# Fourteen pairs of k tiles in place of twelve as seven products each, with other sums and a preparation of four steps

## The chip, the cores and the metric

The kernel runs on one core of one Trainium2 chip. The metric is the time of one execution on the device in microseconds (us), as a median over runs. The profile and the trace come from one further execution with the hardware profiler on. PE is TensorE's matmul, PEld its weight load, DVE is VectorE, ACT is ScalarE, POOL is GpSimd, and SP issues most of the transfers.

## The reference

One decoder layer of 256 tokens and 2048 features in float32: a pair of token mixers (mLSTM and RWKV-7), a cross attention, and a channel mixer. The change lies in the last matrix product, the down projection of the channel mixer:

```python
def conv_glu_ffn(h, w_up, conv_w, conv_b, w_down):
    u = h @ w_up
    uc = conv_b + sum(conv_w[j] * shift_right(u, CONV_WIDTH - 1 - j) for j in range(CONV_WIDTH))
    gate, up = split_cols(uc, (D_FF, D_FF))
    return (jax.nn.gelu(gate, approximate=True) * up) @ w_down
...
h = rms_norm(x, ffn_pre_norm[l])
x = x + rms_norm(conv_glu_ffn(h, ffn_w_up[l], ffn_conv_w[l], ffn_conv_b[l], ffn_w_down[l]), ffn_post_norm[l])
```

The operand of the down projection is 256 x 8192, its weights are 8192 x 2048, and its output is 256 x 2048.

## The kernel before, in words

**Matrix products.** Every float32 operand is split into a high part (a cast to float32r) and a low part (the rest), and a product is made of three: high x high, low x high, high x low. Weights arrive as `raw` tiles of 128x1024 by SP (`Feed.dma`, L428, four buffers). ACT casts the high part (`Feed.hi`, L448, tile `wh`) and DVE subtracts for the low part (`Feed.lo`, L520, tile `wl`), with five buffers of each. All matmuls are issued at L191; nearly all other ACT and DVE instructions pass through the helper `Meter.call`, L68.

**The down projection.** It is two blocks (n = 0 and 1) of 1024 output columns, each over 64 k tiles of 128 rows. A block has four PSUM banks: two halves of 128 tokens by two halves of 512 columns. One k tile costs 4 x 3 = 12 matmuls of 128x512. The operand is kept in `ac`; `asplit` (L1911) splits two k tiles at a time into `as`, first a cast on ACT and then a subtraction on DVE. `as` has two buffers, so the cast for the tiles kk+2 and kk+3 waits until PE is done with the tiles kk-2 and kk-1.

**Pairs.** At the k tiles listed in `SEVEN` (L1906; six in each block) two neighbouring k tiles are multiplied together as a 2x2 by 2x2 product of blocks (two halves of the tokens, two k tiles, two halves of the columns) with seven products in place of eight: `seven_products` (L532) issues 7 x 3 = 21 matmuls in place of 24. Four of them go to extra PSUM banks (`more`), which `join_sums` (L556) combines behind the last pair of a block. The seven products need sums of weights and sums of operands, which `prepare` (L452), a generator, makes in steps. The weights of a pair are loaded to a place of their own (`pair_loads`, L487; `sraw`). That place, the sums `sums` and `f4`, and the joined banks all lie in one SBUF tile, which the trace calls `end`; they are told apart by their shapes and their times. The split sums are the tiles `sa` (of operands), `ts` and `t4` (of weights; the trace calls the last one `t`). `prepare` also overwrites one of the four 512-column quarters of `sraw`, so that the pair's own `wh` and `wl` are split from changed weights.

**Order.** The order of the instructions on each engine is the order in which the code issues them, and each engine works through its own list in that order. For each k tile i, `work` (L577) does the following before it issues the matmuls of tile i:

```python
feed.lo(i + 1 + pair)
...
ahead = b["xs"](k)
if b["seven"]:
    feed.pair_loads(i)
feed.lo(i + 3 + pair)
feed.dma(i + 7 + pair)
if b["seven"]:
    feed.ahead_of_pairs(i)
```

So at tile i the operands for tile i+2 are split (for even i), then the weights of tile i+3 on ACT and on DVE, and behind these comes one step of `prepare` (`ahead_of_pairs`, L492). A pair at tile c is prepared in six steps, one at each of the tiles c-6 to c-1. An entry of `preps` (L402) holds the tile at which the first step is issued.

## Time and profile before

| | |
|---|---|
| runs shown | 1797.34 us median of 3 (1796.83 to 1848.11) |
| profiled execution | 1796.52 us, of which the span of the instructions is 1794.7 us |
| PE busy | 1785.2 us, 99% of the span, 11778 matmuls |
| DVE busy | 1395.6 us, 78% |
| ACT busy | 1076.7 us, 60% |
| granted TensorE clock | 0.999 of full speed, mean |
| down projection | matmuls from 1462.9 us to 1787.0 us |
| transfers of pairs' weights | 24, of 512 KB each |

Matmuls are pipelined, so their durations overlap, and a PE that is busy all the time may still not be at its peak. Times within the text are microseconds from the start of the span; "idle before" is the time in which an engine stood still ahead of an instruction, with the engine whose signal ended it.

### The profile page before, as it was taken

The page shows a single profiled execution, that of the slowest core. Times are in us where ns is not written, and L with a number is a line of the kernel's source. Part 1 is how long each engine was busy: PE and PEld are TensorE (multiplying, and loading weights), DVE is VectorE, ACT ScalarE, POOL GpSimd, SP SyncE. Part 2 cuts the span into 40 slices and gives each one's busy share as a digit, 9 for nine tenths or more (in the row PEclk, how much of TensorE's full clock was granted, in tenths as well). Part 3 has the DMA queues.
Part 4 walks back from the last instruction along what each step waited for, and adds up shares of the span by engine and source line. Part 5 has one row for each costly group of instructions (what it writes and reads, how often), then busy time and mean ns, then how long its engine had stood idle before and what let it go on. Part 6 is the DMA issues. An engine that isn't in the chain of part 4 may idle for free.

```text
span 1794.7 us, 30098 instructions
## 1 busy us (share of the span) xinstructions
PE 1785.2 (99%) x11778; PEld 1629.7 (91%) x11778; DVE 1395.6 (78%) x2020; ACT 1076.7 (60%) x1616; POOL 28.9 (2%) x51
## 2 busy tenths in 40 slices
PE   9999999999999999999999999999999999999998
PEld 9999988888888999999999999999999998888887
DVE  7869995766665767778878777877777778888887
ACT  7576454654554666677566667666655655556554
POOL 0100000000100000000000000000000000000000
PEclk9999999999999999999999999999999999999999
DMA  8755564454556676656666666666666676767664
GB/s 283 206 170 186 164 190 146 125 180 144 200 188 211 227 243 186 190 150 197 208 203 198 203 209 192 199 206 204 199 200 209 192 229 213 227 186 227 209 209 129
DMA packets 99134, 351.59 MB, mean 196 GB/s; under 512 B 10896, under 2 KB 13968, under 8 KB 98864
## 3 DMA queue, kind: packets, MB, share of 16 engines
q1 hardware_dynamic: 97888, 347.38, 61.3%
q8 instruction: 92, 1.51, 0.3%
q0 software_dynamic: 384, 1.18, 0.2%
q10 hardware_dynamic: 720, 1.12, 0.2%
q14 instruction: 50, 0.41, 0.1%
HBM read 347.01 MB, written 2.10 MB: 195 GB/s over the span
## 4 chain that ended last, share of the span: by engine, by line
PE 99%; DVE 0%; DMA 0%; ACT 0%; issue 0%; SPq 0%; DVEq 0%; ACTq 0%
PE fm L191 55%; PE tm L191 37%; PE more L191 2%; PE gram L191 0%; PE Y L191 0%; PE lv L191 0%; DMA op<-in_op_dram 0%; PE X L191 0%; PE num L191 0%; PE zwa L191 0%; PE U L191 0%; PE gramA L191 0%; PE xo L191 0%; PE zg L191 0%; PE Tn L191 0%; PE mT L1472 0%
## 5 line engine op out<-in xcount | busy, mean ns | idle before, releaser
L520 DVE TENSOR_TENSOR wl<-raw,wh 128x1024 fp32r<-128x1024 f32 (+1 forms) x617 | 741.5, 1218 | 128.6 <-ACT wh L448 125.9
L448 ACT CAST wh<-raw 128x1024 fp32r<-128x1024 f32 (+1 forms) x617 | 633.6, 1044 | 112.7 <-PE tm L191 61.7
L191 PE MATMUL fm<-fx,wh 128*128 128x512 f32 (+1 forms) x2240 | 672.8, 364 | 0.6 <-DVE fx L68 0.4
L191 PE MATMUL fm<-fx,wl 128*128 128x256 f32 x2048 | 558.3, 273 | 0.0
L191 PEld LDWEIGHTS fm<-fx,wh 128*128 128x128 f32 x2240 | 409.3, 190 | 49.9 <-DVE fx L68 1.0
L191 PEld LDWEIGHTS fm<-fx,wl 128*128 128x128 f32 x2048 | 393.3, 192 | 0.0
L191 PE MATMUL tm<-wh,as 128*128 128x512 f32 x856 | 254.8, 379 | 0.0
L191 PE MATMUL tm<-wh,hx 128*128 128x512 f32 (+1 forms) x832 | 243.9, 378 | 1.4 <-ACT hx L68 1.4
L191 PEld LDWEIGHTS tm<-wh,as 128*128 128x128 f32 x856 | 161.7, 189 | 23.2 <-DVE as L68 0.3
L68 ACT COPY ul<-fm 128x256 f32<-128x256 f32 x128 | 44.9, 373 | 225.5 <-PE fm L191 225.5
L191 PE MATMUL fm<-hx,wh 128*128 128x256 f32 x1024 | 174.5, 277 | 0.0
L191 PEld LDWEIGHTS tm<-wh,hx 128*128 128x128 f32 x832 | 151.0, 189 | 21.8 <-POOL wh L507 1.6
L191 PE MATMUL tm<-wl,as 128*128 128x512 f32 x428 | 162.2, 379 | 0.0
L191 PEld LDWEIGHTS fm<-hx,wh 128*128 128x128 f32 x1024 | 155.6, 192 | 1.1
L191 PE MATMUL tm<-wl,hx 128*128 128x512 f32 (+1 forms) x416 | 152.5, 373 | 0.4 <-DVE wl L520 0.3
L68 DVE TENSOR_TENSOR us<-fm,ul 128x256 f32<-128x256 f32 x128 | 48.5, 420 | 131.2 <-ACT ul L68 131.2
L191 PE MATMUL fm<-hx,wl 128*128 128x256 f32 x512 | 140.8, 275 | 0.0
L68 ACT CAST as<-ac 128x512 fp32r<-128x512 f32 x64 | 39.4, 617 | 118.8 <-PE tm L191 118.8
L191 PEld LDWEIGHTS fm<-hx,wl 128*128 128x128 f32 x512 | 98.3, 192 | 0.0
L191 PEld LDWEIGHTS tm<-wl,as 128*128 128x128 f32 x428 | 80.9, 189 | 11.5
L191 PEld LDWEIGHTS tm<-wl,hx 128*128 128x128 f32 x416 | 77.5, 189 | 11.2 <-DVE wl L520 0.5
L191 PE MATMUL fm<-mg,wh 128*128 128x512 f32 (+1 forms) x320 | 84.9, 340 | 0.0
(406 smaller groups left out, 2114.8 us busy)
## 6 DMA issues: line engine op xcount, KB each, us to landing
raw<-in_w_fw_dram SPq DMA_DIRECT2D x232, 512.0 KB, 4.3
raw<-in_w_in_dram SPq DMA_DIRECT2D x160, 512.0 KB, 3.7
raw<-in_w_fd_dram SPq DMA_DIRECT2D x104, 512.0 KB, 4.1
raw<-in_w_br_dram SPq DMA_DIRECT2D x32, 512.0 KB, 4.2
raw<-in_w_mw_dram SPq DMA_DIRECT2D x24, 512.0 KB, 4.8
raw<-in_w_fu_dram SPq DMA_DIRECT2D x24, 512.0 KB, 4.0
end<-in_w_fd_dram SPq DMA_DIRECT2D x24, 512.0 KB, 3.6
raw<-in_w_mo_dram SPq DMA_DIRECT2D x8, 512.0 KB, 4.1
```

The lines of the kernel that those rows point to most:

```text
L68: return f(out, *a, **k)
L191: pe.matmul(out, lhsT, rhs, start=start, stop=stop, skip_group_check=True)
L448: nc.scalar.copy(o, v)
L520: nc.vector.tensor_sub(o, v, h)
```

## The change

Three things change, all within the down projection. The reading of the other parts of the program is not touched.

**Pairs.** `SEVEN` goes from six places in each block to seven: 12, 18, 26, 34, 42, 48, 56 and 10, 16, 24, 32, 40, 46, 54. Before, neighbouring pairs were 8 or 10 k tiles apart; now they are 8 apart, or 6 apart at four places (12 to 18 and 42 to 48, 10 to 16 and 40 to 46).

**Other sums.** The seven products are formed from other sums of the same quarters. Two sums of weights are made by one DVE operation of 1024 elements with a broadcast operand; the quarter that is overwritten is the first one, by a sum that needs that operation's result. The products are issued in another order. `join_sums` has two copies on ACT, not one, and four operations on DVE as before.

**Preparation.** It has four steps in place of six, issued at the tiles c-5 to c-2 where there is room, and at c-4 to c-1 where the pair ahead is 6 tiles away (`last + 2`). The first step makes the overwritten quarter, and an assertion says that the pair's weights must not be split before it.

The three places below show the stretch behind the first pair (tiles 12 and 13) of the first block, up to the next pair. Before, the next pair is at tile 20; in the changed kernel it is at tile 18. The numbers behind the names are those of buffers.

DVE before, from the weights of tile 17 (`wl_16088`) to the split of the operands' sums (`sa_16136`): `end` are sums of the preparation of pair 20, `as` operands, `wl_16152` the weights of tile 20.

```order
L520 TENSOR_TENSOR wl_16088<-raw_16009,wh_16086 128x1024
L68 TENSOR_TENSOR end_15830<-end_15830 128x512
L68 TENSOR_TENSOR end_15830<-ac_10740 128x256
L520 TENSOR_TENSOR wl_16106<-raw_16030,wh_16104 128x1024
L68 TENSOR_TENSOR end_15830<-end_15830 128x512
L68 TENSOR_TENSOR end_15830<-ac_10740,end_15830 128x128 x2
L68 TENSOR_TENSOR as_16125<-ac_10740,as_16125 128x512
L520 TENSOR_TENSOR wl_16130<-raw_16056,wh_16128 128x1024
L68 TENSOR_TENSOR end_15830<-end_15830 128x512
L520 TENSOR_TENSOR wl_16152<-end_15830,wh_16150 128x1024
L68 TENSOR_TENSOR end_15830<-end_15830 128x512
L68 TENSOR_TENSOR sa_16136<-end_15830,sa_16135 128x512
```

DVE now, from the first step of the preparation of pair 18, just behind the weights of tile 17, to the split of the operands' sums (`sa_16142`); `wl_16105` and `wl_16134` are the weights of tiles 18 and 19, `ts` the split of two sums of weights.

```order
L68 TENSOR_TENSOR end_15830<-end_15830 128x1024
L68 TENSOR_TENSOR end_15830<-end_15830 128x512
L519 TENSOR_TENSOR wl_16105<-end_15830,wh_16103 128x1024
L68 TENSOR_TENSOR end_15830<-end_15830 128x512
L68 TENSOR_TENSOR end_15830<-ac_10740 128x256
L68 TENSOR_TENSOR as_16128<-ac_10740,as_16128 128x512
L519 TENSOR_TENSOR wl_16134<-end_15830,wh_16132 128x1024
L68 TENSOR_TENSOR end_15830<-end_15830,ac_10740 128x128
L68 TENSOR_TENSOR end_15830<-ac_10740,end_15830 128x128
L68 TENSOR_TENSOR ts_16112<-end_15830,ts_16111 128x1024
L519 TENSOR_TENSOR wl_16160<-raw_16053,wh_16158 128x1024
L68 TENSOR_TENSOR sa_16142<-end_15830,sa_16141 128x512
```

Before, three steps of sums stand ahead of the first weights of the pair (`wl_16152`), and `sa` follows them with one more sum between. Now the first weights of the pair come directly behind the first step, and `sa` stands behind the weights of tile 20.

ACT in the same stretch before: `wh_16128` is tile 19, `wh_16150` tile 20, `wh_16179` tile 21.

```order
L448 CAST wh_16086<-raw_16009 128x1024
L448 CAST wh_16104<-raw_16030 128x1024
L68 CAST as_16125<-ac_10740 128x512
L448 CAST wh_16128<-raw_16056 128x1024
L68 CAST sa_16135<-end_15830 128x512
L448 CAST wh_16150<-end_15830 128x1024
L68 CAST ts_16158<-end_15830 128x1024
L68 CAST as_16175<-ac_10740 128x512
L448 CAST wh_16179<-end_15830 128x1024
```

And now: `wh_16083` is tile 17, `wh_16103` and `wh_16132` are the pair's tiles 18 and 19, `wh_16158` is tile 20.

```order
L450 CAST wh_16083<-raw_16009 128x1024
L450 CAST wh_16103<-end_15830 128x1024
L68 CAST ts_16111<-end_15830 128x1024
L68 CAST as_16128<-ac_10740 128x512
L450 CAST wh_16132<-end_15830 128x1024
L68 CAST t4_16113<-end_15830 128x512
L68 CAST sa_16141<-end_15830 128x512
L450 CAST wh_16158<-raw_16053 128x1024
```

The pair's first weights, `wh_16103`, are now the second instruction behind the operands of tile 16, and the cast of the operands' sums (`sa_16141`) stands ahead of the weights of tile 20.

PE at the pair, with what each matmul waits for. Before, from the first product of pair 20:

```order
L191 MATMUL more<-wh,as 128x512 [waits Activation_49]
L191 MATMUL more<-wh,as 128x512 [waits DVE_49]
L191 MATMUL more<-wl,as 128x512
L191 MATMUL tm<-wh,as 128x512 [waits Activation_49]
L191 MATMUL tm<-wh,as 128x512
L191 MATMUL tm<-wl,as 128x512 [waits DVE_49]
L191 MATMUL more<-wh,sa 128x512 x2
L191 MATMUL more<-wl,sa 128x512
L191 MATMUL tm<-wh,sa 128x512 x2
L191 MATMUL tm<-wl,sa 128x512
L191 MATMUL more<-ts,sa 128x512 x2
L191 MATMUL more<-ts,sa 128x512 [waits DVE_49]
```

Now, from the first product of pair 18:

```order
L191 MATMUL tm<-wh,as 128x512 [waits Activation_49]
L191 MATMUL tm<-wh,as 128x512 [waits DVE_49]
L191 MATMUL tm<-wl,as 128x512 [waits DVE_49]
L191 MATMUL more<-wh,as 128x512 x2
L191 MATMUL more<-wl,as 128x512
L191 MATMUL tm<-wh,sa 128x512 [waits Activation_49]
L191 MATMUL tm<-wh,sa 128x512 [waits DVE_49]
L191 MATMUL tm<-wl,sa 128x512
L191 MATMUL more<-wh,sa 128x512 x2
L191 MATMUL more<-wl,sa 128x512
L191 MATMUL more<-ts,sa 128x512 x6
L191 MATMUL tm<-t_16113,as 128x512 x2
```

In both, the first two products use the plain operands `as`, and the third is the first that uses `sa`. Now that third product waits for ACT (the high part of `sa`) and then for DVE (the low part).

The diff:

```diff
--- before.py
+++ after.py
@@ -393,12 +393,13 @@
             a, g = blocks[0]["srcs"], blocks[1]["srcs"]
             self.src = a[:LEAD] + [c for p in zip(a[LEAD:], g) for c in p] + g[len(a) - LEAD:]
             self.src += [s for b in blocks[2:] for s in b["srcs"]]
-            n, self.pairs, self.preps = sum(len(b["srcs"]) for b in blocks[:2]), {}, []
+            n, self.pairs, self.preps, self.summed = sum(len(b["srcs"]) for b in blocks[:2]), {}, [], set()
             for b in blocks[2:]:
                 if b["seven"]:
                     for k in b["seven"]["at"]:
                         self.pairs[n + k], self.pairs[n + k + 1] = 0, 1
-                        self.preps.append([n + k - 6, self.prepare(n + k, k), n + k, []])
+                        last = self.preps[-1][2] if self.preps else 0
+                        self.preps.append([max(n + k - 5, last + 2), self.prepare(n + k, k), n + k, []])
                 n += len(b["srcs"])
             self.raw, self.st, self.nd, self.ns, self.nl, self.nop = {}, {}, 0, 0, 0, 0
 
@@ -442,6 +443,7 @@
         def hi(self, upto):
             while self.ns <= min(upto, len(self.src) - 1):
                 self.dma(self.ns)
+                assert self.pairs.get(self.ns) != 0 or self.ns in self.summed
                 r = self.raw[self.ns]
                 wh = self.staged("wh", r)
                 for o, v in self.pieces(self.ns, wh, r):
@@ -451,30 +453,27 @@
 
         def prepare(self, c, k):
 
-            raw, t, f = M["sraw"], M["sums"], M["f4"]
-            (b11, b12), (b21, b22) = ([raw[:, i, j * 512:j * 512 + 512] for j in range(2)] for i in range(2))
+            raw, t, f = M["sraw"].rearrange("p i (j n) -> p (i j) n", j=2), M["sums"], M["f4"]
             x = acpair(k).rearrange("p k (t s) -> p (k t) s", t=2)
-            dve.tensor_add(t[:, 0:512], b22, b12)
+            dve.tensor_add(t[:, 0:1024].rearrange("p (j n) -> p j n", j=2), raw[:, 0:1].broadcast_to((P, 2, 512)), raw[:, 1:3])
+            dve.tensor_add(raw[:, 0], t[:, 0:512], raw[:, 2])
+            self.summed.add(c)
+            yield
+            dve.tensor_add(t[:, 1024:], raw[:, 0], raw[:, 3])
             dve.tensor_sub(f[:, 0:2], x[:, 1:2].broadcast_to((P, 2, P)), x[:, 0:4:3])
-            yield
-            dve.tensor_sub(b12, b12, b11)
-            dve.tensor_sub(f[:, 2], x[:, 0], f[:, 1])
-            dve.tensor_sub(f[:, 3], x[:, 2], f[:, 2])
-            yield
-            dve.tensor_add(t[:, 512:1024], b22, b12)
-            sa = [T2("sa", [P, 4, P], F32R) for _ in range(2)]
-            M["sa"].append(sa)
-            act.copy(sa[0], f)
-            yield
-            dve.tensor_sub(t[:, 1024:], b21, t[:, 512:1024])
-            dve.tensor_sub(sa[1], f, sa[0])
             ts, t4 = [C("ts", f"bg{j}", [P, 1024], F32R) for j in range(2)], [T2("t4", [P, 512], F32R) for _ in range(2)]
             M["ts"].append((ts, t4))
             act.copy(ts[0], t[:, 0:1024])
             yield
+            dve.tensor_sub(f[:, 2], f[:, 1], x[:, 0])
+            dve.tensor_add(f[:, 3], x[:, 2], f[:, 2])
             dve.tensor_sub(ts[1], t[:, 0:1024], ts[0])
+            sa = [T2("sa", [P, 4, P], F32R) for _ in range(2)]
+            M["sa"].append(sa)
             act.copy(t4[0], t[:, 1024:])
-            yield
+            act.copy(sa[0], f)
+            yield
+            dve.tensor_sub(sa[1], f, sa[0])
             dve.tensor_sub(t4[1], t[:, 1024:], t4[0])
             yield
 
@@ -539,13 +538,13 @@
         half = lambda w, c: [v[:, 0, c * 512:c * 512 + 512] for v in w]
         tops = lambda c: [v[:, c * 512:c * 512 + 512] for v in t]
         old, more = banks, sv["more"]
-        for n, (o, x, w) in enumerate(((more[0], [v[:, 0] for v in a], half((w0h, w0l), 0)),
-                                       (old[0], [v[:, 2] for v in a], half((w1h, w1l), 0)),
-                                       (more[2], [v[:, 1] for v in sa], half((w0h, w0l), 1)),
-                                       (old[1], [v[:, 3] for v in sa], half((w1h, w1l), 1)),
-                                       (more[3], [v[:, 0] for v in sa], tops(0)),
-                                       (more[1], [v[:, 2] for v in sa], tops(1)),
-                                       (old[2], [v[:, 3] for v in a], t4))):
+        for n, (o, x, w) in enumerate(((old[1], [v[:, 2] for v in a], half((w1h, w1l), 1)),
+                                       (more[0], [v[:, 0] for v in a], half((w0h, w0l), 1)),
+                                       (old[0], [v[:, 3] for v in sa], half((w1h, w1l), 0)),
+                                       (more[1], [v[:, 2] for v in sa], half((w0h, w0l), 0)),
+                                       (more[2], [v[:, 1] for v in sa], tops(0)),
+                                       (more[3], [v[:, 0] for v in sa], tops(1)),
+                                       (old[3], [v[:, 3] for v in a], t4))):
             wh, wl = (turns(v) for v in w)
             mm(o, x[0], wh, start=new and o in more, stop=False)
             mm(o, x[1], wh, start=False, stop=False)
@@ -557,13 +556,14 @@
 
         more, s = sv["more"], [M["join"][:, i] for i in range(4)]
         sv["sums"] = s
-        act.copy(s[0], more[0])
-        dve.tensor_add(s[2], s[0], more[1])
-        yield
-        dve.tensor_add(s[1], s[2], more[2])
-        dve.tensor_add(s[2], s[2], more[3])
-        yield
-        dve.tensor_add(s[3], s[1], more[3])
+        act.copy(s[1], more[0])
+        dve.tensor_add(s[3], s[1], more[1])
+        yield
+        act.copy(s[0], more[2])
+        dve.tensor_sub(s[0], s[0], s[3])
+        dve.tensor_sub(s[3], s[3], more[3])
+        yield
+        dve.tensor_add(s[2], s[0], more[3])
         yield
 
     def run():
@@ -1903,7 +1903,7 @@
         fu = block("fm", W("w_fw", f - 6), fu_xs(f), fw_evac(f), cols=256, wide=lambda k: M["fx"][:, :, k])
 
     M["as"], M["a4"], M["sa"], M["ts"] = {}, [], [], []
-    SEVEN = [12, 20, 30, 38, 48, 56], [10, 18, 28, 36, 46, 54]
+    SEVEN = [12, 18, 26, 34, 42, 48, 56], [10, 16, 24, 32, 40, 46, 54]
 
     def acpair(e):
         return M["ac"][e // 16][:, e % 16:e % 16 + 2] if e < 32 else M["ac"][2 + (e - 32) // 8][:, e % 8:e % 8 + 2]
```

## The prediction

> **What bounds the kernel now.** I read the page first, then the busy times of the down projection's two blocks.

> ```profile
> PE 1785.2 (99%) x11778; PEld 1629.7 (91%) x11778; DVE 1395.6 (78%) x2020; ACT 1076.7 (60%) x1616; POOL 28.9 (2%) x51
> PE 99%; DVE 0%; DMA 0%; ACT 0%; issue 0%; SPq 0%; DVEq 0%; ACTq 0%
> 1463.08:1624.00 160.92, 160.92 (x748) 140.91 (x747) 135.92 (x168) 96.09 (x120) 0.00 (x0) 1.00 0.69 217
> 1624.00:1777.60 153.60, 153.60 (x713) 134.52 (x712) 132.89 (x164) 92.53 (x119) 0.00 (x0) 1.00 0.64 199
> ```

> The first row gives each engine's busy time, the second the shares of the chain that ended last. The others are stretches: length, then busy us of PE, PEld, DVE and ACT with counts, POOL, the granted clock, DMA. PE is busy in 160.92 of 160.92 us and in 153.60 of 153.60, at clock 1.00: it waits for nobody, so here a matmul less is time less, and any wait that appears is time more. DVE is busy 135.92 / 160.92 = 84% and 87%, which is not much room for engines that depend on each other.

> What a matmul costs comes from the chain, in which PE's runs are merged:

> ```profile
> 1498.05 16.19 PE tm L191 x75
> ```

> 16.19 / 75 = 0.216 us from one matmul to the next (the 379 ns of one matmul overlap). A k tile takes 12 x 0.216 = 2.59 us, a pair 21 x 0.216 = 4.53.

> **What the change removes.** Two pairs more, three matmuls each: 6 x 0.216 = 1.30 us less PE. That is all that PE gains. It has fourteen pairs for certain: the order has 21 matmuls at each.

> **What it adds to DVE.** The added pairs bring their sums and splits. Their prices:

> ```profile
> L68 DVE TENSOR_TENSOR end<-end x48: 680/684/687, 1481.4 to 1755.7; 128x512 f32<-128x512 f32 x48
> L68 DVE TENSOR_TENSOR end<-ac,end x24: 280/288/294, 1484.1 to 1751.8; 128x128 f32<-128x128 f32 x24
> L68 DVE TENSOR_TENSOR end<-ac x12: 415/418/421, 1482.0 to 1749.4; 128x256 f32<-128x256 f32 x12
> L68 DVE TENSOR_TENSOR sa<-end,sa x12: 680/683/686, 1488.9 to 1756.3; 128x512 fp32r<-128x512 f32 x12
> L68 DVE TENSOR_TENSOR ts<-end,ts x12: 1217/1219/1221, 1491.8 to 1759.2; 128x1024 fp32r<-128x1024 f32 x12
> L68 DVE TENSOR_TENSOR t<-end,t x12: 681/684/686, 1494.1 to 1761.5; 128x512 fp32r<-128x512 f32 x12
> ```

> Before, a pair costs 4 x 0.684 + 2 x 0.288 + 0.418 + 0.683 + 1.219 + 0.684 = 6.32 us of DVE. Now two of the four sums are one operation of 1024 elements. The trace has none such on `end`; by the row of `ts` it takes 1.22 us, against 1.37 for two. Its broadcast operand should not matter: an addition of 256 elements with a broadcast operand is in the 0.418 row, at the price that its size gives beside 0.288 for 128 and 0.684 for 512. So a pair now costs 6.17 us, 14 of them 86.3 against 75.8 us. Spread over the stage that would be hidden (DVE idles some 45 us in it). It is not spread: over six k tiles, a pair included, PE needs 4.53 + 4 x 2.59 = 14.9 us, and DVE 6 x (1.22 + 0.34) for the tiles' `wl` and half an `as` plus 6.17, 15.5 us. At the four places where pairs are 6 apart DVE has no slack left, so the order of its work there decides.

> **The walk between two pairs.** The stretch of the trace in which the two pairs at tiles 12 and 20 are prepared shows how the engines are geared:

> ```profile
> 1494.00 0.59 PE L191 MATMUL more<-wh,as 128*128 128x512 f32 x2
> 1495.08 0.41 PEld L191 LDWEIGHTS more<-wh,sa 128*128 128x128 f32 x2
> 1498.54 0.59 PE L191 MATMUL tm<-wh,as 128*128 128x512 f32 x2
> ```

> ```profile
> 1498.73 0.62 ACT L68 CAST as<-ac 128x512 fp32r<-128x512 f32 x1 [1.97 <-PE tm L191]
> 1499.26 1.99 ACT L448 CAST wh<-raw 128x1024 fp32r<-128x1024 f32 x2
> 1503.91 0.62 ACT L68 CAST as<-ac 128x512 fp32r<-128x512 f32 x1 [2.67 <-PE tm L191]
> 1504.44 1.04 ACT L448 CAST wh<-raw 128x1024 fp32r<-128x1024 f32 x1
> 1505.39 0.61 ACT L68 CAST sa<-end 128x512 fp32r<-128x512 f32 x1
> 1507.37 1.05 ACT L68 CAST ts<-end 128x1024 fp32r<-128x1024 f32 x1 [0.41 <-DVE end L68]
> ```

> ```profile
> 1499.39 0.69 DVE L68 TENSOR_TENSOR as<-ac,as 128x512 fp32r<-128x512 f32 x1 [1.17 <-ACT as L68]
> 1500.33 1.23 DVE L520 TENSOR_TENSOR wl<-raw,wh 128x1024 fp32r<-128x1024 f32 x1 [0.26 <-ACT wh L448]
> 1501.48 0.68 DVE L68 TENSOR_TENSOR end<-end 128x512 f32<-128x512 f32 x1
> 1502.08 0.42 DVE L68 TENSOR_TENSOR end<-ac 128x256 f32<-128x256 f32 x1
> 1502.41 1.22 DVE L520 TENSOR_TENSOR wl<-raw,wh 128x1024 fp32r<-128x1024 f32 x1
> 1504.15 0.61 DVE L68 TENSOR_TENSOR end<-ac,end 128x128 f32<-128x128 f32 x2
> 1504.68 0.69 DVE L68 TENSOR_TENSOR as<-ac,as 128x512 fp32r<-128x512 f32 x1
> 1506.66 0.68 DVE L68 TENSOR_TENSOR end<-end 128x512 f32<-128x512 f32 x1
> ```

> The first fence is PE: pair 12 starts at 1494.00 and ends at 1498.54. The cast of the operands for tile 16 starts 0.19 behind that end, because its buffer is released by it; everything on ACT and DVE is queued behind it. DVE reaches the first step of the next preparation at 1501.48, 2.94 us behind the end of the pair. From one DVE instruction to the next, with no wait between, are 1.14 us for 1024 elements, 0.60 for 512, 0.33 for 256; on ACT 0.95 for 1024 and 0.52 for 512 (1504.44 to 1505.39, 1503.91 to 1504.44). A signal between ACT and DVE takes 0.04 (1506.66 + 0.68 = 1507.34, the cast of `ts` starts at 1507.37); an instruction that needs the one ahead of it on DVE starts some 0.03 behind its end (two of 0.288 in 0.61).

> Now the changed order behind pair 12, in us after its end; nothing up to 2.94 is changed. First step: sum of 1024 at 2.94, then the overwritten quarter, which needs it, from 4.19 to 4.87. The pair's first weights (tile 18) may be cast only now: ACT stands idle from 1.76, casts `wh` from 4.91 to 5.95, and DVE, which has `wl` of tile 18 next in its list, stands idle from 4.87 to 5.99. Behind it come the sums of 512 at 7.13 and 256 at 7.73, and `as` of tile 18 at 8.07 (its cast stands behind those of `wh` and `ts`: 6.80 to 7.42). `wl` of tile 19 runs from 8.67, the two operand sums from 9.81 to 10.42. Only then can ACT cast `sa`: 10.46 to 11.07, and behind it `wh` of tile 20: 10.98 to 12.02. DVE has `wl` of tile 20 next, 12.06 to 13.28, and the low part of `sa` behind that, 13.20 to 13.88.

> PE is at pair 18 at 4 x 2.59 = 10.37. The weight load of the low `sa` is the second of the third product. In pair 12 the two loads of that product start at 1495.08, 1.08 us into the pair, and the second 0.22 later: it is due at 10.37 + 1.30 = 11.67. It can start at 13.92. **PE stands 2.25 us**, where it stood for nothing before. The low `t4` follows at 13.80 to 14.48, while PE needs it at its seventh product, at 10.37 + 18 x 0.216 + 2.25 = 16.5: no second wait. Nor is there a debt to the next pair: tile 20 starts at 17.15, `wl` of tile 22 ends near 17.4, and the next cast of operands waits for PE again, as at 1498.73.

> The other three places (42 to 48, 10 to 16, 40 to 46) have the same rows in the same order. At the pairs 8 apart the first step stands at c-5, with a k tile more of time. By the same walk, the low `sa` is ready 0.7 us before those pairs start, 2 us before it is due. Four places cost 4 x 2.25 = 9.0 us.

> The price of one place is bounded so. If each link were at its shortest (no 0.03 and 0.04, the 1024 sum at 1.14, no overlap lost), it would be 1.8; with another 0.3 us of lateness at the first step, 2.6. Zero is excluded by nothing but the walk, and is a rival.

> **Edits at no cost.** The loads of a pair:

> ```profile
> 1488.43 0.33 SPq L487 DMA_DIRECT2D end<-in_w_fd_dram  x1
> 1491.93 0.33 SPq L487 DMA_DIRECT2D end<-in_w_fd_dram  x1
> DMA to landing us min/median/max: 3.4/3.6/6.7
> ```

> They are issued when the `wl` of the pair ahead have read the place; in the new order that is no later, and 1491.93 + 3.6 = 1495.5 is 6.0 us ahead of the step that needs them (2.9 with the slowest landing). SP's queue stands behind them for the same two events as before; four more loads are pair loads, four fewer `raw`. The second copy in `join_sums` (0.58 us on ACT) and the new order of its sums lie behind a block's last pair, where ACT idles 2.2 us a cycle; uncovered, both copies would cost 1.2 us. The first products of a pair now need the weights of its second tile, ready at 9.89 of 10.37; if late, that would add to a wait that comes anyway.

> **Sum.** -1.30 + 9.0 = +7.7 us. From the profiled execution's 1796.52 (span 1794.7) that gives 1804.2. The runs shown lie at 1796.83 and 1797.34, 0.3 to 0.8 above it; with 0.5 added I predict 1804.7 us, and for this case alone 1803 to 1806.5.

> **Rivals.** (a) *The wait is covered*, and only the six matmuls count: 1796.52 + 0.5 - 1.30 = 1795.7 us. The place is the low `sa`; the gain decides if it is ready by 11.67, 2.25 us before the walk has it. For it: DVE idles 1.17 us ahead of 1499.39, and PE has had no wait in twelve preparations. Against: that idle time lies ahead of the cast that PE releases and can't be used, and in all twelve the pair ahead was 8 tiles away or more. (b) *Part of the wait*, 1 us a place, if ACT or DVE gets through the list faster where they wait for each other: +2.7, 1799.7 us. The walk has DVE idle for 1.1 us ahead of `wl` of tile 18 and 0.6 ahead of that of tile 20; these are the only links that could shrink so. (c) *A wait drags the clock down.* PE's rows show

> ```profile
> 1789.00:1792.00 3.00, 0.93 (x2) 0.10 (x1) 1.59 (x4) 0.58 (x1) 0.00 (x0) 1.00 0.69 252
> 1792.00:1794.70 2.70, 0.00 (x0) 0.00 (x0) 0.00 (x0) 0.00 (x0) 0.00 (x0) 0.67 0.31 114
> 7.76 0.95 PE L191 MATMUL tm<-wh,hx 128*128 128x296 f32 x4 [1.38 <-ACT hx L68]
> 5.00:10.00 5.00, 3.53 (x23) 2.75 (x22) 3.15 (x9) 2.57 (x7) 1.16 (x2) 1.00 1.00 377
> ```

> The clock falls to 0.67 in the last stretch, some 2 us after PE's last matmul; a wait of 1.38 us left it at 1.00. If each wait of 2.25 us put the other 16 matmuls of its pair (3.5 us) at 0.67, each would cost 1.7 us more: +6.8, 1811.5 us. [...]

> **How the numbers follow.** The forecast 0.66, (a) 0.15, (b) 0.15, (c) 0.04. The range, 1795.2 to 1807.5, holds the forecast with four waits of up to 2.6 us and a run's own spread, (b) and (a); (c) is left out. All cases lie within 1% of the time before, well inside the 2% that a measurement of this kernel can about tell from no change: faster 0.01, same 0.98, slower 0.01, the outer two for causes that I don't see.

> **What would show it.** PE has 11772 matmuls. In the list of PE's waits four new ones on DVE's `sa`, near 2.2 us each, at tiles 18 and 48 of the first block and 16 and 46 of the second, and none at the ten other pairs. ACT waits some 3 us for DVE's `end` ahead of the first `wh` of these pairs. If these waits are missing or below 1 us, the walk is wrong in the links between ACT and DVE; if they are there and the time isn't longer, my price for the matmuls is.

## The result, and the profile after

| | before | changed |
|---|---|---|
| median of 6 runs | 1796.83 us | 1808.91 us (1805.82 to 1811.2) |
| ratio | | 1.0066, interval 1.0051 to 1.0081 |
| profiled execution, span | 1796.52, 1794.7 us | 1806.3, 1804.2 us |

One of the six runs before was a slow one, at 1848.11 us, and the ratio leaves it out.

The changed kernel is slower, by 9 to 14 us. The prediction, 1804.7 us in a range of 1795.2 to 1807.5, had the direction of its number right and the size too small: the median lies above the range. The six runs fall into two groups, three at 1805.8 to 1806.8 and three at 1811.0 to 1811.2. That there are groups turns out to be the part that the prediction had put aside.

The page after, first the span and the busy times, then the waits of PE in the whole span (us in total, times, longest):

```profile
span 1804.2 us, 30109 instructions
PE 1786.8 (99%) x11772; PEld 1629.4 (90%) x11772; DVE 1406.4 (78%) x2026; ACT 1081.2 (60%) x1624; POOL 28.6 (2%) x51
```

```profile
PE tm L191 <- DVE sa L68: 7.6, 4, 1.9
PE tm L191 <- ACT hx L68: 1.8, 1, 1.8
```

PE has the six matmuls less, and four new waits on DVE's `sa`. The same place as in the prediction, behind the first pair, on DVE and then on ACT:

```profile
1499.77 0.69 DVE L68 TENSOR_TENSOR as<-ac,as 128x512 fp32r<-128x512 f32 x1 [1.17 <-ACT as L68]
...
1501.86 1.94 DVE L68 TENSOR_TENSOR end<-end 128x1024 f32<-128x1024 f32 x2
1504.91 1.23 DVE L519 TENSOR_TENSOR wl<-end,wh 128x1024 fp32r<-128x1024 f32 x1 [1.11 <-ACT wh L450]
...
1509.05 0.29 DVE L68 TENSOR_TENSOR end<-ac,end 128x128 f32<-128x128 f32 x1
...
1510.97 1.22 DVE L519 TENSOR_TENSOR wl<-raw,wh 128x1024 fp32r<-128x1024 f32 x1 [0.50 <-ACT wh L450]
1512.11 0.68 DVE L68 TENSOR_TENSOR sa<-end,sa 128x512 fp32r<-128x512 f32 x1
```

```profile
1503.83 1.04 ACT L450 CAST wh<-end 128x1024 fp32r<-128x1024 f32 x1 [3.15 <-DVE end L68]
...
1509.37 0.62 ACT L68 CAST sa<-end 128x512 fp32r<-128x512 f32 x1 [1.56 <-DVE end L68]
1509.90 1.04 ACT L450 CAST wh<-raw 128x1024 fp32r<-128x1024 f32 x1
```

Pair 12 ends at 1498.92 here (the cast that it releases starts 0.20 later, at 1499.12). Counted from there, the first step starts at 2.94, ACT casts the pair's first weights at 4.91, and the low `sa` runs from 13.19 to 13.87. The prediction had 2.94, 4.91 and 13.20 to 13.88.

What the prediction lacked shows on PE. Two of the four pairs, from the second product to the seventh:

```profile
1509.93 0.59 PE L191 MATMUL more<-wh,as 128*128 128x512 f32 x2
...
1512.85 0.48 PE L191 MATMUL tm<-wh,sa 128*128 128x512 f32 x1 [1.90 <-DVE sa L68]
...
1514.71 2.46 PE L191 MATMUL more<-ts,sa 128*128 128x512 f32 x6
1517.02 0.81 PE L191 MATMUL tm<-t,as 128*128 128x512 f32 x3
...
1588.89 0.59 PE L191 MATMUL more<-wh,as 128*128 128x512 f32 x2
...
1591.81 0.48 PE L191 MATMUL tm<-wh,sa 128*128 128x512 f32 x1 [1.90 <-DVE sa L68]
...
1594.29 0.81 PE L191 MATMUL tm<-t,as 128*128 128x512 f32 x3
```

Without a wait, five products lie between these two starts, 5 x 3 x 0.216 = 3.24 us. The second of the pairs takes 1594.29 - 1588.89 = 5.40, so its wait costs 2.16 us. The first takes 7.09: 2.16 and another 1.69. Its six matmuls on `ts` take 2.46 us, where the same six took 1.46 before, at pair 12:

```profile
1496.59 1.46 PE L191 MATMUL more<-ts,sa 128*128 128x512 f32 x6
```

The stretches of time around them (length, busy us of PE, PEld, DVE, ACT and POOL with counts, granted clock, DMA) say why:

```profile
1509.00:1512.80 3.80, 1.95 (x10) 1.36 (x8) 3.27 (x6) 3.43 (x5) 0.00 (x0) 1.00 0.91 355
1512.80:1514.00 1.20, 1.15 (x4) 0.96 (x5) 1.20 (x3) 0.55 (x1) 0.00 (x0) 0.72 0.76 123
1514.00:1515.00 1.00, 1.00 (x4) 0.82 (x3) 1.00 (x1) 0.00 (x0) 0.00 (x0) 0.50 0.76 307
1515.00:1516.00 1.00, 1.00 (x4) 0.73 (x4) 1.00 (x2) 0.00 (x0) 0.00 (x0) 0.50 0.17 70
1516.00:1517.00 1.00, 1.00 (x4) 0.86 (x3) 0.27 (x1) 0.00 (x0) 0.00 (x0) 0.63 0.84 160
1517.00:1518.50 1.50, 1.50 (x8) 1.32 (x7) 0.00 (x0) 0.58 (x2) 0.00 (x0) 1.00 0.82 284
1590.00:1596.00 6.00, 4.19 (x19) 3.70 (x20) 5.39 (x7) 3.12 (x5) 0.00 (x0) 1.00 0.69 206
```

The granted clock was at 0.50 behind the first wait, from 1513.3 (the second row's mean of 0.72 is 1.00 up to there and 0.50 behind) to 1516.7: 3.41 us in the trace's record, so 1.7 us of work lost. Behind the second wait it stayed at 1.00.

So the profiled execution adds up: -1.30 for the matmuls, 4 x 2.16 = +8.64, +1.69 for the clock, and +0.4 by which the down projection starts later (the wait on `hx` at the kernel's start was 1.8 us, 1.4 before): +9.4, against 1804.2 - 1794.7 = +9.5 us.

### The profile page after: what moved, and what is told of

The parts are those of the page before. It is cut to its first block, busy times and chain, and to the rows that moved or that the text cites. A ratio compares the mean times of both kernels' runs of the same rounds, so it can differ in the third digit from the quotient of the medians.

```text
span 1804.2 us, 30109 instructions
## 1 busy us (share of the span) xinstructions
PE 1786.8 (99%) x11772; PEld 1629.4 (90%) x11772; DVE 1406.4 (78%) x2026; ACT 1081.2 (60%) x1624; POOL 28.6 (2%) x51
## 4 chain that ended last, share of the span: by engine, by line
PE 98%; DVE 1%; ACT 0%; DMA 0%; issue 0%; SPq 0%; DVEq 0%; ACTq 0%
PE fm L191 55%; PE tm L191 36%; PE more L191 2%; PE gram L191 0%; PE Y L191 0%; DMA op<-in_op_dram 0%; PE lv L191 0%; PE X L191 0%; PE num L191 0%; ACT wh L450 0%; PE zwa L191 0%; PE U L191 0%; PE gramA L191 0%; PE xo L191 0%; PE zg L191 0%
## 5 line engine op out<-in xcount | busy, mean ns | idle before, releaser
L191 PE MATMUL fm<-fx,wh 128*128 128x512 f32 (+1 forms) x2240 | 672.8, 364 | 0.6 <-DVE fx L68 0.4
L191 PE MATMUL fm<-fx,wl 128*128 128x256 f32 x2048 | 558.3, 273 | 0.0
L191 PEld LDWEIGHTS fm<-fx,wh 128*128 128x128 f32 x2240 | 409.3, 190 | 49.9 <-DVE fx L68 1.0
L191 PEld LDWEIGHTS fm<-fx,wl 128*128 128x128 f32 x2048 | 393.2, 192 | 0.0
L191 PE MATMUL tm<-wh,as 128*128 128x512 f32 x828 | 246.5, 379 | 0.0
L191 PE MATMUL tm<-wh,hx 128*128 128x512 f32 (+1 forms) x832 | 243.9, 378 | 2.0 <-ACT hx L68 1.8
L68 ACT COPY ul<-fm 128x256 f32<-128x256 f32 x128 | 44.8, 373 | 225.2 <-PE fm L191 225.2
L191 PEld LDWEIGHTS tm<-wh,as 128*128 128x128 f32 x828 | 156.4, 189 | 22.5 <-DVE as L68 0.3
L191 PE MATMUL fm<-hx,wh 128*128 128x256 f32 x1024 | 174.5, 277 | 0.0
L191 PEld LDWEIGHTS tm<-wh,hx 128*128 128x128 f32 x832 | 151.1, 189 | 22.6 <-POOL wh L506 2.0
L191 PE MATMUL tm<-wl,as 128*128 128x512 f32 x414 | 156.9, 379 | 0.0
L191 PEld LDWEIGHTS fm<-hx,wh 128*128 128x128 f32 x1024 | 155.5, 192 | 1.1
L191 PE MATMUL tm<-wl,hx 128*128 128x512 f32 (+1 forms) x416 | 152.5, 373 | 0.0
L68 DVE TENSOR_TENSOR us<-fm,ul 128x256 f32<-128x256 f32 x128 | 48.4, 420 | 131.2 <-ACT ul L68 131.2
L191 PE MATMUL fm<-hx,wl 128*128 128x256 f32 x512 | 140.8, 275 | 0.0
L191 PEld LDWEIGHTS fm<-hx,wl 128*128 128x128 f32 x512 | 98.3, 192 | 0.0
L68 ACT CAST as<-ac 128x512 fp32r<-128x512 f32 x64 | 39.4, 617 | 95.6 <-PE tm L191 95.6
L191 PEld LDWEIGHTS tm<-wl,as 128*128 128x128 f32 x414 | 78.2, 189 | 11.1
L191 PEld LDWEIGHTS tm<-wl,hx 128*128 128x128 f32 x416 | 77.5, 189 | 10.7 <-DVE wl L519 0.3
L191 PE MATMUL fm<-mg,wh 128*128 128x512 f32 (+1 forms) x320 | 84.9, 340 | 0.0
```

The lines of the kernel that those rows point to most:

```text
L68: return f(out, *a, **k)
L191: pe.matmul(out, lhsT, rhs, start=start, stop=stop, skip_group_check=True)
```

## The experiments

Theory 1: the waits come from the order of the two lists at the four places 6 tiles apart, and the rest of the loss from the clock. The rivals: the other sums or products cost by themselves; six tiles are too few for DVE. Differences below are between the medians of the kernel and of the kernel before on the same chip.

**All pairs 8 apart, seven in each block.** The changed kernel with

```diff
-    SEVEN = [12, 18, 26, 34, 42, 48, 56], [10, 16, 24, 32, 40, 46, 54]
+    SEVEN = [8, 16, 24, 32, 40, 48, 56], [6, 14, 22, 30, 38, 46, 54]
```

> The changed kernel with its fourteen pairs set 8 k tiles apart everywhere (8, 16, ... 56 and 6, 14, ... 54); sums and steps as changed. Theory 1 (the waits come from the four places 6 tiles apart, where the preparation starts a tile late): no wait of PE on sa, no clock at 0.5 inside the work, and the time of before less six matmuls of 0.216 us, -1.3 us (+-0.6). Theory 2 (the other sums or the new order of products make PE wait, wherever the pairs stand): waits on sa remain at several pairs, and the time is above that of before.

Measured: 1797.59 us (1796.26 to 1800.06), +0.8, and not -1.3. No wait on `sa`, but another one, in the profiled execution of 1800.06 us:

```profile
PE tm L191 <- ACT wh L450: 1.0, 1, 1.0
PE tm L191 <- DVE wl L519: 0.6, 1, 0.6
```

Both are at the second block's first pair, tile 6. On DVE, the first step of its preparation stands in the midst of the first block's results (`z` and the sums read from `tm`), and the weights of that pair behind them:

```profile
1629.89 0.68 DVE L68 TENSOR_TENSOR z<-end 128x512 f32<-128x512 f32 x1
1630.50 1.23 DVE L519 TENSOR_TENSOR wl<-raw,wh 128x1024 fp32r<-128x1024 f32 x1
1631.64 1.95 DVE L68 TENSOR_TENSOR end<-end 128x1024 f32<-128x1024 f32 x2
1633.51 0.68 DVE L68 TENSOR_TENSOR end<-tm,end 128x512 f32<-128x512 f32 x1
...
1637.39 0.68 DVE L68 TENSOR_TENSOR z<-end 128x512 f32<-128x512 f32 x1
1637.99 1.22 DVE L519 TENSOR_TENSOR wl<-end,wh 128x1024 fp32r<-128x1024 f32 x1
```

The clock fell as well, to 0.50 from 1643.9 to 1647.3 us; one stretch of it:

```profile
1644.00:1646.00 2.00, 2.00 (x6) 1.61 (x5) 2.00 (x4) 1.21 (x2) 0.00 (x0) 0.50 0.73 236
```

In this execution it also fell at the kernel's start, from 8.9 to 12.3 us. So the expectation failed by a new wait of my own making; the places that were to be tested were silent. The clean form of it is the next.

**All pairs 8 apart, none where a block is drained.** Seven and six pairs:

```diff
-    SEVEN = [12, 18, 26, 34, 42, 48, 56], [10, 16, 24, 32, 40, 46, 54]
+    SEVEN = [8, 16, 24, 32, 40, 48, 56], [10, 18, 26, 34, 42, 50]
```

> The changed kernel with all pairs 8 tiles apart, seven in the first block (8 to 56) and six in the second (10 to 50), so that no pair of the second block is prepared while the sums of the first block are still drained, as it was at tile 6. Theory 1: no wait of PE on ACT or DVE in the down projection and no lost clock; thirteen pairs, three matmuls less than before, -0.65 us (+-0.4), all executions within 1 us of each other. Rival (pairs 8 apart wait as well, and tile 6 was only the place where it showed): waits on sa or wl at other pairs, slower than before.

Measured: 1795.91 us (1795.57 to 1796.44), -0.81, and PE waits for nothing in the down projection. Theory 1 holds; a pair 8 tiles behind another waits nowhere.

**The twelve old places.** The changed kernel with `SEVEN` as before:

> The changed kernel with the twelve places of before; sums, order of products and the four steps as changed. Theory 1: no wait, twelve pairs, so the time of before within 0.6 us; DVE is some 12 x 0.15 = 1.8 us less busy than before, which nobody waits for. Theory 2 (sums or products cost by themselves): slower than before by over 1 us, with a wait that the trace names.

Measured: 1796.8 us, +0.04 (ratio 1.0, 0.999 to 1.001), no wait. The other sums, the new order of products and the four steps cost nothing by themselves. One part of the expectation was wrong: over the 314.6 us of the stage, DVE is no less busy, although it has twelve instructions fewer. The row of this kernel, and that of the kernel before:

```profile
1463.30:1777.90 314.60, 314.60 (x1459) 275.40 (x1458) 269.42 (x319) 189.40 (x241) 0.00 (x0) 1.00 0.65 209
```

```profile
1463.08:1777.68 314.60, 314.60 (x1460) 275.43 (x1458) 268.89 (x331) 188.61 (x239) 0.00 (x0) 1.00 0.66 208
```

**Operand sums one step earlier.** The changed kernel at its own fourteen places; in `prepare` the last two sums of operands go from the third step to the second, and the low `sa` from the fourth to the third, ahead of `ts`:

```diff
 dve.tensor_sub(f[:, 0:2], x[:, 1:2].broadcast_to((P, 2, P)), x[:, 0:4:3])
+dve.tensor_sub(f[:, 2], f[:, 1], x[:, 0])
+dve.tensor_add(f[:, 3], x[:, 2], f[:, 2])
...
-dve.tensor_sub(f[:, 2], f[:, 1], x[:, 0])
-dve.tensor_add(f[:, 3], x[:, 2], f[:, 2])
-dve.tensor_sub(ts[1], t[:, 0:1024], ts[0])
 sa = [T2("sa", [P, 4, P], F32R) for _ in range(2)]
 M["sa"].append(sa)
-act.copy(t4[0], t[:, 1024:])
 act.copy(sa[0], f)
-yield
+act.copy(t4[0], t[:, 1024:])
 dve.tensor_sub(sa[1], f, sa[0])
+dve.tensor_sub(ts[1], t[:, 0:1024], ts[0])
+yield
```

> The changed kernel at its own places; the last two sums of operands are made one step earlier, and the split of sa follows one step earlier, ahead of the weights of tile 20. Walked in the same way as in the prediction (us behind the end of the pair ahead): operand sums done 8.7, sa cast 8.7 to 9.3, wl of tile 19 9.2 to 10.4, low sa 10.3 to 11.0, due 11.67. Theory 1 (only the place of sa in the two lists is late): no wait on sa, none of over 0.3 us on wl of the pair, -1.3 us against before (+-0.6). Theory 3 (six tiles are too few for DVE's 15.5 us of work, wherever sa stands): the wait moves to wl or ts and stays above 1 us at each of the four places, so slower than before by 3 us or more.

Measured: 1795.46 us (1795.07 to 1796.27; before 1796.32 to 1797.44 in 31 runs), -1.30, no wait of PE at all in the stage. The row that decides, on DVE behind the first pair, which ends at 1498.78 here:

```profile
1509.23 0.69 DVE L68 TENSOR_TENSOR sa<-end,sa 128x512 fp32r<-128x512 f32 x1
```

That is 10.45 to 11.14 behind the pair, where 10.3 to 11.0 was expected and 11.67 is due. The rival that six tiles are too few for DVE has fallen: the same work at the same places fits when the two operand sums, the cast of `sa` and the split of `sa` stand higher in the lists.

**Six steps at the new places.** The kernel before with only `SEVEN` changed.

> The kernel before (its sums, its products, its six steps) with only the fourteen new places. The first step of a pair 6 tiles behind another is issued at that pair itself, two tiles ahead of where the four steps start. By the walk, sa is ready at 8.2 us behind the pair ahead, due at 11.7, wl of the pair's second tile at 9.9 of 10.6. Theory 1 (the late start and the order of the four steps make the wait): no wait on sa, -1.3 us against before (+-0.6). Theory 3 (six tiles are too few for the work): waits at the four places, slower than before by 2 us or more.

Measured: 1795.19 us (1794.67 to 1796.12), -1.57, no wait. The places alone are harmless too. It takes both, the places 6 apart and the four steps that start two tiles later there with `sa` at their end.

**`sa` ahead of the weights of tile 20.** The changed kernel; at the tile ahead of a pair, the step comes first:

```diff
+if b["seven"] and i + 1 in feed.pairs:
+    feed.ahead_of_pairs(i)
 feed.lo(i + 3 + pair)
```

> The changed kernel, but at the tile ahead of a pair the step of the preparation is issued ahead of the weights of tile 20, not behind them; only the four places 6 tiles apart differ. By the walk the low sa is ready at 12.2 us, not 13.9, due 11.67: PE is late by 0.5 us at each place. Theory 1: four waits on sa of under 0.6 us, no clock at 0.5 inside the work, -1.3 + 4 x 0.5 = +0.7 us against before (+-0.6). Rival: the wait stays above 1.5 us, since something other than the list's order holds sa back.

Measured: 1797.61 us (1796.46 to 1797.91), +1.06. The waits of the weight loads and of PE:

```profile
PEld tm L191 <- DVE sa L68: 2.3, 4, 0.6
PE tm L191 <- DVE sa L68: 0.7, 4, 0.2
```

The loads are late by 0.6 us four times, as the walk has it (0.5). Moving that step past one instruction is worth 8.4 us, the lost clock included (1806.05 of the changed kernel on the same chip, below, against 1797.61).

**The same with a longer wait.** At the four places the split of `ts` is done twice, ahead of `sa`:

```diff
+if late:
+    dve.tensor_sub(ts[1], t[:, 0:1024], ts[0])
 dve.tensor_sub(sa[1], f, sa[0])
```

> As the kernel with sa ahead of the weights of tile 20, and at the four places one more DVE operation of 1024 elements (a split done twice, same result) ahead of sa: each wait grows by 1.14 us to a lateness of 1.65, of which PE stands still some 1.4. Theory W (halved only where PE stood still over some 1.8 us of one window of 3.41): no stretch at half the clock in any execution, -1.3 + 4 x 1.65 = +5.3 us (+-1), all executions alike. Rival S (any wait above 1 us can halve it): executions differ by steps of 1.7 us and some lie at +7 or more.

Measured: 1802.59 us (1802.05 to 1802.8), +6.0, five executions alike.

```profile
PE tm L191 <- DVE sa L68: 5.8, 4, 1.4
```

Two of the places, as stretches:

```profile
1511.00:1516.00 5.00, 3.81 (x18) 3.35 (x19) 5.00 (x7) 2.59 (x4) 0.00 (x0) 1.00 0.40 134
1588.00:1592.00 4.00, 2.99 (x14) 2.64 (x15) 4.00 (x6) 1.98 (x3) 0.00 (x0) 1.00 0.41 112
```

Four waits in which PE stood still 1.44 us each, and the clock at 1.00 behind all of them. Only the waits are paid.

**The changed kernel again.**

> The changed kernel unchanged, for more executions beside those of the same chip. Four waits of 2.16 us each and the six matmuls make +7.3 us; each stretch of 3.41 us at half the clock adds 1.7. Theory W (the granted clock is judged in windows of 3.41 us at fixed times, and is halved for the next window where PE stood still for over some 1.8 us of one; a wait of 1.9 us does that or not, by where the windows happen to lie): executions fall in levels about 1.7 us apart, from +7.3 (none) to +14.1 us (four), and not one value. Rival P (the clock fell at the first of the four places for a cause of that place): each execution loses it once, +9 us always.

Measured: 1805.01, 1805.05, 1806.05, 1810.12 and 1810.92 us, at mean clocks of 1.0, 1.0, 0.999, 0.997 and 0.996. By these clocks (0.001 is 1.8 us) the executions lost no stretch, none, one at most, two or three, and four. Rival P has fallen. The profiled execution is the last of these, with the same four waits of 1.9 us, and all four lost the clock:

```profile
1513.00:1517.20 4.20, 4.20 (x13) 3.39 (x12) 2.82 (x3) 0.00 (x0) 0.00 (x0) 0.59 0.70 209
1591.50:1595.70 4.20, 4.20 (x12) 3.40 (x13) 3.29 (x4) 0.37 (x1) 0.00 (x0) 0.59 0.67 177
1676.80:1681.00 4.20, 4.20 (x14) 3.37 (x13) 2.79 (x3) 0.00 (x0) 0.00 (x0) 0.59 0.65 203
1755.30:1759.50 4.20, 4.20 (x12) 3.39 (x13) 3.26 (x4) 0.34 (x1) 0.00 (x0) 0.59 0.65 176
```

0.59 over 4.2 us is 3.41 us at 0.5, 1.7 us each time. -1.30 + 8.64 + 4 x 1.71 = +14.2 is the span's 1808.8 - 1794.7 = +14.1. By the same sum an execution without any loss would be at +7.3, near 1804; the two at 1805.0 lie 1 us above that, which stays open.

**Longer waits.** The changed kernel with the same split done twice.

> The changed kernel with the same additional DVE operation ahead of sa at the four places: each wait grows by 1.14 us to a lateness of 3.3, of which PE stands still 3.0. Theory W: the standing still lies for over 1.8 us in one window unless a window's border cuts it near its middle, some 0.56 of 3.41 us of all positions, so three or four of the four waits halve the clock: -1.3 + 13.2 + 3 or 4 x 1.7 = +17 to +18.7 us, at times +15.3. Rival R (a wait must fill a whole window of 3.41 us): no stretch at half the clock, +11.9 us. [...]

Measured: 1812.35, 1817.99, 1818.24 and 1818.35 us. PE stood still 3.04 us at each place. In the profiled execution, 1812.35, only the first and the third of the four halved the clock. That is fewer than theory W expected, and more than the none of rival R. It was run twice more for its trace:

> The kernel with the longer wait once more, for its trace: three of its four executions were at 1818 us, 3 us above what four waits of 3.3 us and four windows at half the clock make (-1.3 + 13.2 + 4 x 1.7 = +15.3), at a mean clock of 0.994. If a single wait can cost two windows, the trace of such an execution shows five or six stretches at clock 0.5 inside the work. If not, it shows four, and PE's waits are longer than 3.04 us there. An execution at 1812 us has two stretches and tells nothing new.

> The kernel with the longer wait a third time, for the trace of an execution at 1818 us. Theory W as before gives four stretches at clock 0.5 at most, one for each wait, so at most +18.7 us. If one wait can cost two windows, the trace shows five or six. An execution at 1810 or 1812 us has one or two and leaves this open.

Measured: 1810.15 and 1810.4 us, each with the clock halved at the third place only; -1.3 + 4 x 3.30 + 1.7 = +13.6 is about what 1810.15 is above the kernel before (+13.4); 1810.4 was on another chip, 12.4 above a single execution of the kernel before. In the third, the stretches at the first and at the third place:

```profile
1508.00:1518.00 10.00, 6.96 (x33) 5.79 (x32) 8.85 (x12) 4.96 (x7) 0.00 (x0) 1.00 0.66 215
1670.00:1680.00 10.00, 6.96 (x26) 5.53 (x25) 9.18 (x11) 4.10 (x6) 0.00 (x0) 0.83 0.69 217
```

The same wait of 3.04 us loses the clock or not. In the trace's record of the granted clock, every stretch at 0.5 begins at a whole multiple of 3.4133 us after the record's first entry (1508.69 us, 442 multiples, in the first trace of the changed kernel; 442, 465, 490 and 513 multiples in the execution with four). These are the borders, and what lies between two of them is a window. So the 24 waits of six traces can be cut:

| PE still, within one window of 3.41 us at most | waits | clock halved behind |
|---|---|---|
| 1.90 to 3.04 us, ending 0.16 us or more ahead of the border, or across it | 9 | 9 |
| 1.90 us, ending 0.02 and 0.05 us ahead of the border | 2 | 0 |
| 1.09 to 1.75 us (waits of 1.44, 1.90 and 3.04 us) | 13 | 0 |

Theory W holds for these but for the two that ended just ahead of a border. For the longer wait it expected three or four losses and the traces have two, one and one, because the borders lay near the middle of most waits. It does not hold for the three executions at 1818 us. Four losses, the most it allows, make +18.7 (the +15.3 in the first of the two expectations above is a slip in the sum); these are at +21.4 to +21.8. Their mean clock of 0.994 says that 10 to 11.8 of their 1816 us were lost. Of that, 0.4 to 2.0 us can lie behind the last matmul, as in the traces here. What is left is about five or six stretches, more than there are waits. Either a single wait can cost two, or the clock fell at another place too. No trace of such an execution was taken, so this stays open.

**Fifteen pairs.** The kernel with the operands' sums a step earlier, and

```diff
-    SEVEN = [12, 18, 26, 34, 42, 48, 56], [10, 16, 24, 32, 40, 46, 54]
+    SEVEN = [8, 14, 22, 28, 36, 42, 50, 56], [10, 16, 24, 30, 38, 46, 54]
```

> The kernel with the operands' sums a step earlier, with fifteen pairs: 8, 14, 22, 28, 36, 42, 50, 56 and 10, 16, 24, 30, 38, 46, 54, so that six places are 6 tiles apart, each followed by one of 8. If the order in the lists is the whole cause and a place of 8 repays what a place of 6 borrows from DVE: no wait, nine matmuls less than before, -1.9 us (+-0.5). If DVE's 15.5 us of work in 14.9 us add up from place to place: waits on wl or as behind the second or third such place, and no gain over fourteen pairs.

Measured: 1795.02 us (1794.67 to 1795.43; before 1796.38 to 1797.66 in 19 runs), -1.70, no wait, nine matmuls fewer. This kernel, the six steps at the new places and the operands a step earlier are lower than both kernels in all their runs, which don't overlap with those of the kernel before on the same chip, though the intervals of their ratios just reach 1 (0.9981 to 1.0 for fifteen pairs, up to 1.0001 and 1.0002 for the other two).

## Why the prediction was wrong

*The six matmuls, -1.30 us.* Right: -1.30 with the operands a step earlier, -0.81 for three (0.65), -1.70 for nine (1.94). That the first agrees to the hundredth is luck: the six-step kernel, with the same six matmuls less, is at -1.57.

*The walk.* Right to 0.01 us in its rows, at the four places named and nowhere else. One wait was put at 2.25 us and cost 2.16; the four weight loads waited 9.2 us, 2.30 each. That the cause is the place of `sa` in the two lists was argued there; moving it, by one instruction or by one step, has shown it.

*DVE without slack.* Overstated, though the sum did not use it. The 15.5 us against 14.9 add up whole durations. By the prediction's own 1.14, 0.60 and 0.33 us from one start to the next, the same work is some 14.4 us (an estimate), and the kernel with fifteen pairs has six places 6 tiles apart without a wait.

*The edits at no cost.* Right: the kernel at the twelve old places is 0.04 us off. The price of DVE per pair was not: one operation in place of two saved nothing on DVE.

*The clock.* Here it failed. The step was rival (c), with a chance of 0.04, and the sum left it out. The row of 1.38 us at clock 1.00, the longest wait of PE in the trace of before, agreed with that and could not decide; that a wait of 2.25 us leaves the clock at 1.00 too was the author's assumption, and no run shows it for all of the waits. The runs put 1.7 us on none to all four of the waits, by where the windows lay: 0 to 6.8 us. That (c) had the same price is chance: it reckoned with 3.5 us at 0.67, and measured are 3.41 us at 0.50. With -1.30 + 8.64 as its base the forecast was the case of no loss, the lowest of what could be measured, and its range ended at 1807.5 though its own rival (c) stood at 1811.5; three of the six runs are at 1811.0 to 1811.2.

The view that (c) was read from held more than was taken from it. Its 0.67 is the mean of a stretch of 2.70 us that began at 1.00: in the trace's record the clock was at 0.50 from 1792.9 on. PE's last two matmuls in that trace:

```profile
1788.80 1.13 PE L191 MATMUL sum<-z,turn 128*128 128x512 f32 x2 [0.91 <-ACT turn L68]
```

They end at 1789.93. So the clock fell 3.0 us behind them, not some 2: less than 3.41 us without a matmul had been enough.

The mechanism that makes PE wait was right; the term that was missing from the sum is the second price of the same waits.

The borders lie at another time in each of the two traces: the record's first entry is 4.32 us behind the start of the span in that of the kernel before and 4.63 us in that of the changed kernel. Of the waits with 1.90 us or more within one window, nine of eleven halved the clock.

*The runs.* I added 0.5 us from the profiled execution to the runs' median and took one number; with losses of 1.7 us at a time the median of six (1808.91) falls between two groups and is no execution's time. That the kernel would stay within 2% of the time before (0.98) was right, but the interval of 1.0051 to 1.0081 tells far smaller changes from none than the prediction thought.

## What to carry to other kernels

When a step of preparation is put off, walk the in-order lists of all engines from the last event that didn't move; the work may fit in the time, as it did here, and still be late by its place in the list. A wait that appears on a TensorE that was never idle can have two prices: its own length, and, where some 1.9 us of it or more fell into one window of 3.41 us, in nine cases of eleven here, a window at half the clock behind it. The range of a forecast must hold both. An instruction that the next product needs goes ahead of one that is needed a tile later.

## What the runs showed of the hardware

The clock also fell behind two waits in one window: at the second block's first pair of the kernel with pairs at tile 6, they were 1.05 and 0.56 us, with two matmuls between them, and the clock was at 0.50 from 1643.9 on. So the length of a single wait doesn't decide alone; what is counted is open.

A change of -0.07% in PE's matmuls became +0.4% by its four waits, and +0.5 to +0.8% with the clock, which differs from execution to execution.
